# A last stage with TensorE in program order, DRAM writes issued by ScalarE, gelus kept in groups of four and four more early down tiles

## Chip, cores and metric

The kernel runs on one core of a Trainium2 chip. The metric is the device time of one execution in microseconds (us).

## What is computed

One decoder layer on 512 tokens of width 1024: a token mixer (mLSTM heads and sliding-window attention), cross-attention to 256 memory tokens, and a PEER layer with 16,384 single-neuron experts. Nearly all that matters here is the PEER layer. Cut to its core:

```python
qh = (xb @ w_pq).reshape(T, P_HEADS, 2, P_KEY_DIM)
s1 = einsum('thd,nd->thn', qh[:, :, 0], sub_keys1)
s2 = einsum('thd,nd->thn', qh[:, :, 1], sub_keys2)
v1, i1 = top_k(s1, 16); v2, i2 = top_k(s2, 16)
# best 16 of the 16 x 16 sums, per token and head
top_s, pos = top_k(cand_s, 16)
eidx = take_along_axis(cand_i, pos, -1)
g = softmax(top_s)
a = gelu(einsum('thkd,td->thk', expert_down[eidx], xb))
out = einsum('thkd,thk->td', expert_up[eidx], g * a)
```

A residual add and a final RMSNorm follow.

## The kernel before

The PEER layer is computed in two ways. For the first block of 128 tokens the kernel gathers the chosen rows of `expert_down` and `expert_up` with 256 indirect DMAs (`gather`, a Python generator that the code advances with `step`), and VectorE multiplies and sums them. The other three blocks (384 tokens) are computed densely, for all 16,384 experts in 128 tiles of 128:

- A **down tile** (class `Down`) loads 128 experts' weights (`draw`, two tiles per DMA), ScalarE casts them to a high part `dh`, VectorE subtracts to get a low part `dl`, TensorE runs 24 matmuls of 384 columns into `acc_d` (two PSUM buffers), and ScalarE takes the gelu.
- An **up tile** (`up_tile`, `up_mm`) loads the weights `uraw` (two tiles per DMA) and casts them to `uh` (ScalarE) and `ul` (VectorE). VectorE multiplies the gelu by the dense gates `wt` to get `cf`, which is split into `ch` (ScalarE) and `cl` (VectorE). TensorE runs 18 matmuls of 512 columns that add to six PSUM accumulators `acc_u` over all tiles. `uh`, `ul`, `ch` and `cl` have two buffers each.

Down tiles need only the layer's input, so `SP` = 68 of them are **early** (`Early.fill`): they are spread as filler for TensorE over the top-k (`peer_topk`, by the table `FRT`, and `FEND` columns at its end) and over `gating`, in which ScalarE and VectorE make one-hot matrices and TensorE multiplies them into the gates (`w`). The gelus of early tiles go to DRAM in groups of four (`gd<-gsp`) and come back later (`gsr<-gd`). The gates go to DRAM as eight writes of 2 MB (`wd<-stg`). In the kernel before, both kinds of writes are issued by SyncE, in one queue with the loads.

After gating `LEAD` = 5 down tiles are made, with 8 gather steps (`GLD`) among them. The **last stage** is the loop over `up_order()`: per up tile it first makes the down tiles that `made_by(u)` asks for, then the up tile, then some gather steps. Fresh gelus stay in a ring of 10 tiles. Then `finish` adds the residual, normalizes and writes out.

A scheduler of the framework sets each engine's order of instructions by its own timing model, within the data dependences and buffer counts. Each engine then runs its order strictly one after the other.

Of the kernel before, what the change touches and what calls it, by code (L numbers as in the profile page):

```python
# [11 lines left out]
F32 = mybir.dt.float32  # L12
# [9 lines left out]
P = 128  # L22
D = 1024
# [16 lines left out]

UG = 4
FRT = [16] + [20] * 14 + [24]
FEND = 3 * KT
FGT0 = KT
FGT = 3
SP = (sum(FRT) + FEND + FGT0 + (ND - NS) * 32 * FGT) // KT
# [2 lines left out]


GQ = range(9, 32, 2)
GLD = 8
GST = 122

LEAD = 5
RING = 10

# [604 lines left out]
def gating(c, early, ga):  # L664

    nc, ps, gs, mp = c.nc, c.ps, c.gs, c.mp
    V, A, T = nc.vector, nc.scalar, nc.tensor
    for b in range(NG + NS, NB):
        tr = []
        for n_, src in (("I1T", c.I1), ("I2T", c.I2), ("gT", c.gg)):  # L670
            tp = ps.tile([P, 512], F32, tag="a", name="tp_i")
            tr_ = T.transpose(tp[:, :P], src[:, b].rearrange("p h k -> p (h k)"), c.ident)
            o = gs.tile([P, P], F32, tag=n_, bufs=1, name=n_)
            A.copy(o, tp[:, :P])
            tr.append(o)
        i1, i2, g = tr
        n1 = gs.tile([P, P], F32, tag="n1", bufs=1, name="n1")
        A.mul(n1, i1, -1.0)
        io = c.iota.unsqueeze(1).to_broadcast([P, 4, P])

        def onehot(q):

            o1 = gs.tile([P, 4, P], F32, tag="oh1", bufs=5, name="oh1")
            ib = i1[:, 4 * q:4 * q + 4].unsqueeze(2).to_broadcast([P, 4, P])
            if q % 2:
                V.tensor_tensor(o1, io, ib, op=ALU.is_equal)
            else:
                for t1 in range(4):
                    t = 4 * q + t1
                    A.activation(o1[:, t1], c.iota, AF.Abs, bias=n1[:, t:t + 1])  # L690
                A.activation(o1, o1, AF.Relu, bias=1.0, scale=-1.0)
            return o1

        oh = [onehot(q) for q in range(3)]
        if b == NG + NS:
            with c.tc.issue_after(tr_.ins):
                early.fill(FGT0)
        for q in range(32):
            if q % 8 == 0:
                stg = gs.tile([P, NK, 32], F32, tag="stg", bufs=2, name="stg")  # L700
            if q + 3 < 32:
                oh.append(onehot(q + 3))
            o1 = oh[q]
            w = ps.tile([P, 512], F32, tag="b", name="w")
            w4 = w.rearrange("p (i t) -> p i t", t=4)
            for t1 in range(4):
                t = 4 * q + t1
                o2 = gs.tile([P, P], F32, tag="oh2", bufs=4, name="oh2")
                last = V.tensor_scalar(o2, c.iota, i2[:, t:t + 1], g[:, t:t + 1], op0=ALU.is_equal, op1=ALU.mult)
                mm = T.matmul(w4[:, :, t1], o1[:, t1], o2, start=True, stop=True)  # L710
            q8 = q % 8
            A.copy(stg[:, :, 4 * q8:4 * q8 + 4], w4)
            if q8 == 7:
                nc.sync.dma_start(c.wd[b - NG][:, :, 32 * UG * (q // 8):32 * UG * (q // 8 + 1)].rearrange("g p i -> p g i"),
                                  stg.rearrange("p (g i) t -> p g (i t)", i=UG))
            with c.tc.issue_after(mm.ins):
                early.fill(FGT)
            if b == NB - 1 and q in GQ:
                with c.tc.issue_after(c.sc[HD - 1][-1].ins), c.tc.issue_after(last.ins):
                    step(ga, 1)  # L720


def gather(c):

    nc, gp, mp = c.nc, c.gp, c.mp
    V, A, G = nc.vector, nc.scalar, nc.gpsimd
    dots = gp.tile([P, P], F32, name="dots")
    c.gacc = gp.tile([P, D], F32, name="gacc")

    def fetch(src, j):  # L730
        r = gp.tile([P, D], F32, tag="rows", bufs=8, name="rows")
        G.indirect_dma_start(out=r, out_offset=None, in_=src,  # L732
                             in_offset=bass.IndirectOffsetOnAxis(ap=c.eidx[:, j:j + 1], axis=0))
        return r

    for j in range(P):
        r = fetch(c.a["down_r"], j)
        V.tensor_tensor_reduce(r, r, c.xn0, 1.0, 0.0, op0=ALU.mult, op1=ALU.add, accum_out=dots[:, j:j + 1])  # L738
        yield
    coef = gp.tile([P, P], F32, name="coef")  # L740
    A.activation(coef, dots, AF.Gelu)
    V.tensor_tensor(coef, coef, c.gg[:, 0].rearrange("p h k -> p (h k)"), op=ALU.mult)
    for j in range(P):
        r = fetch(c.a["up"], j)
        if j == 0:
            V.tensor_scalar(c.gacc, r, coef[:, j:j + 1], None, op0=ALU.mult)
        else:
            V.scalar_tensor_tensor(c.gacc, r, coef[:, j:j + 1], c.gacc, op0=ALU.mult, op1=ALU.add)  # L748
        yield


def split3(c, pool, raw, tag, bufs):
    hi = pool.tile([P, D], F32R, tag=tag + "h", bufs=bufs, name=tag + "h")
    lo = pool.tile([P, D], F32R, tag=tag + "l", bufs=bufs, name=tag + "l")
    c.nc.scalar.copy(hi, raw)  # L755
    return hi, lo
# [25 lines left out]
class Down:  # L782
# [27 lines left out]
    def out(self):  # L810
        c = self.c
        i2 = self.i2
        if i2 >= SP:
            g = c.gl.tile([P, TD], F32, tag="gel", bufs=RING, name="gel")
            c.nc.scalar.activation(g, self.acc[:, :TD], AF.Gelu)
            return g
        if i2 % UG == 0:
            c.gsp = c.dp.tile([P, UG, TD], F32, tag="gsp", bufs=2, name="gsp")
        c.nc.scalar.activation(c.gsp[:, i2 % UG], self.acc[:, :TD], AF.Gelu)
        if i2 % UG == UG - 1:  # L820
            c.nc.sync.dma_start(c.gd[i2 // UG], c.gsp)
        return None


def up_tile(c, u, i2, gel, acc):
# [9 lines left out]
            c.gsr = c.gl.tile([P, UG, TD], F32, tag="gsr", bufs=2, name="gsr")  # L835
            nc.sync.dma_start(c.gsr, c.gd[i2 // UG])
    if i2 % GRP == 0:
        c.uraw = up.tile([P, GRP, D], F32, tag="uraw", bufs=2, name="uraw")
        nc.sync.dma_start(c.uraw, c.a["up"].rearrange("(i p) d -> p i d", p=P)[:, i2:i2 + GRP])
    g = c.gsr[:, i2 % UG] if i2 < SP else gel[i2]  # L840
    raw = c.uraw[:, i2 % GRP]
    last = u == NK - 1
    if last:
        z = c.xlo.rearrange("p k t -> p (k t)")
        hi, lo = z[:, 0:D], z[:, D:2 * D]
        A.copy(hi, raw)
    else:
        hi, lo = split3(c, up, raw, "u", 2)
    V.tensor_tensor(lo, raw, f32(hi), op=ALU.subtract)  # L849
    cf = up.tile([P, TD], F32, tag="cf", bufs=2, name="cf")  # L850
    if last:
        ch, cl = z[:, 2 * D:2 * D + TD], z[:, 3 * D:3 * D + TD]
    else:
        ch = up.tile([P, TD], F32R, tag="ch", bufs=2, name="ch")
        cl = up.tile([P, TD], F32R, tag="cl", bufs=2, name="cl")
    c.cf = V.tensor_tensor(cf.rearrange("p (b t) -> p b t", t=32), g.rearrange("p (b t) -> p b t", t=32),
                    c.wt.rearrange("p b (q i t) -> p (b q) i t", q=4, i=UG)[:, :, i2 % UG], op=ALU.mult)
    A.copy(ch, cf)  # L858
# [204 lines left out]
def body(tc, a, out, dbg=None):  # L1063
# [3 lines left out]
    with ExitStack() as st:  # L1067
        def pool(name, bufs=1, side="left", **k):
            return tc.tile_pool(name=name, bufs=bufs, side=side, reuse_waits="tile", **k)
# [45 lines left out]
        def ahead(n):  # L1115
            for _ in range(n):
                gel.append(Down(c, len(gel)).mm().out())
# [5 lines left out]
            ws.close()  # L1123
        c.gl = st.enter_context(pool("gels"))
        with pool("gather", side="right") as c.gp:
            ga = gather(c)
            with pool("gating") as c.gs:
                gating(c, early, ga)
            c.up = st.enter_context(pool("up"))
            assert len(gel) == SP  # L1130
            for n in range(LEAD):
                ahead(1)
                with tc.issue_after(c.dl.ins):
                    step(ga, GLD * (n + 1) // LEAD - GLD * n // LEAD)
            pst_ = [c.ps.tile([P, 512], F32, tag=t, name="acc_u") for t in "bbbbaa"]
            acc = [[pst_[2 * b], pst_[2 * b + 1]] for b in range(ND)]
            last = []
            g0 = len(GQ) + GLD

            due = [u + made_by(u) for u in range(-1, GST)]  # L1140
            rows = [(2 * P - g0) * (d - due[0]) // (due[-1] - due[0]) for d in due]
            rows += [rows[-1]] * (NK - GST)
            for u, i2 in enumerate(up_order()):
                ahead(made_by(u) - len(gel))
                parts = up_tile(c, u, i2, gel, acc)
                for i in range(rows[u + 1] - rows[u]):
                    with tc.issue_after((c.cf if i == 0 else c.cl).ins):
                        step(ga, 1)
                if u >= NK - 2:
                    last.append(parts)  # L1150
                else:
                    for b in range(ND):
                        up_mm(c, u, parts, acc, b)
            step(ga, 2 * P)
            c.hb = []
            for b in range(NB):
                c.hb.append(c.gp.tile([P, D], F32, tag="rows", bufs=8, name="hb"))
                nc.sync.dma_start(c.hb[b], c.hd[b])
            c.gfin = c.xn0
            nc.scalar.dma_start(c.gfin, a["prow"][0, 0:D].partition_broadcast(P))  # L1160
# [79 lines left out]
```

## Time and profile before

| | |
|---|---|
| runs of the kernel before | 1663.74 us median (1662.36 to 1670.41, three runs) |
| the profiled execution | 1663.32 us; its span from first to last instruction 1661.6 us |
| busy in the span | TensorE 97%, VectorE 74%, ScalarE 43%, GpSimd 36% |
| chain that ended last | TensorE 89%, VectorE 5% |
| mean granted TensorE clock | 0.992 |

The table is read thus: TensorE is almost always busy and nearly all of the chain runs through it, so a change can gain only what TensorE now waits or runs at a lower clock, some 3% at most, unless it removes matmuls. Which waits those are must be read stage by stage.

### The profile page before, as it was taken

Reading aid. Unit: us, or ns where it says so; the run is one execution under the profiler, and the core shown is the slowest. Engines: PE = TensorE matmul, PEld = TensorE weight load, DVE = VectorE, ACT = ScalarE, POOL = GpSimd, SP = SyncE. Lnnn points to the kernel's source line nnn. Section 1 sums busy time; section 2 is a strip of 40 time slices with the busy share of each in tenths; the row PEclk is TensorE's granted clock in tenths of the full one; section 3 lists DMA queues with packets and bytes.
Section 4 is the critical chain, followed back from the end, with each engine's and each line's share of the span. In section 5 each row is a group of like instructions: output and inputs, shape, how many; then the busy total and the mean of one; then the engine's idle time right before and its main releaser. Section 6 shows DMA issues by size and latency. Waiting matters only on the chain.

```text
span 1661.6 us, 22993 instructions
## 1 busy us (share of the span) xinstructions
PE 1613.3 (97%) x8367; PEld 1415.6 (85%) x8368; DVE 1224.1 (74%) x2686; ACT 722.1 (43%) x1209; POOL 599.1 (36%) x427
## 2 busy tenths in 40 slices
PE   7998899999999999999998999999999999999987
PEld 5766688878999999899997988888888888888865
DVE  5545565464787887877877778778778878887995
ACT  5435544343544454677743333333333333333333
POOL 2000000000027878877333244434434444443630
PEclk9999999999999999999999999999999999999998
DMA  5236135232255435678999989889899899987992
GB/s 214 76 127 253 62 116 178 76 152 106 96 166 146 115 71 140 178 197 223 376 306 406 348 311 368 321 335 348 314 357 366 296 353 357 342 326 260 394 368 101
DMA packets 149969, 400.58 MB, mean 241 GB/s; under 512 B 28240, under 2 KB 62176, under 8 KB 137440
## 3 DMA queue, kind: packets, MB, share of 16 engines
q1 hardware_dynamic: 90096, 255.76, 42.2%
q0 software_dynamic: 55360, 134.32, 24.3%
q10 hardware_dynamic: 4400, 9.04, 1.5%
q8 instruction: 65, 1.06, 0.3%
q14 instruction: 48, 0.39, 0.1%
HBM read 356.28 MB, written 42.80 MB: 240 GB/s over the span
## 4 chain that ended last, share of the span: by engine, by line
PE 89%; DVE 5%; issue 3%; ACT 2%; DMA 1%; POOL 0%; DVEq 0%; POOLq 0%; ACTq 0%
PE acc_d L806 10%; PE acc_d L805 10%; PE acc_d L804 10%; PE acc_u L871 9%; PE acc_u L872 9%; PE acc_u L870 9%; PE acc_f L970 4%; PE acc_f L972 4%; PE acc_f L971 4%; PE w L710 3%; PE acc_t L984 2%; PE acc_t L985 2%; PE acc_t L983 2%; DVE ul L849 1%; PE s L550 1%
## 5 line engine op out<-in xcount | busy, mean ns | idle before, releaser
L804 PE MATMUL acc_d<-xhi,dh 128*128 128x384 f32 x1024 | 351.2, 343 | 5.7 <-ACT dh L755 4.7
L806 PE MATMUL acc_d<-xhi,dl 128*128 128x384 f32 x1024 | 346.2, 338 | 1.7 <-DVE dl L793 1.7
L805 PE MATMUL acc_d<-xlo,dh 128*128 128x384 f32 x1024 | 344.9, 337 | 0.0
L871 PE MATMUL acc_u<-ul,ch 128*128 128x512 f32 x762 | 298.4, 392 | 2.7 <-DVE ul L849 2.7
L872 PE MATMUL acc_u<-uh,cl 128*128 128x512 f32 x762 | 297.7, 391 | 0.0
L655 POOL DMA_INDIRECT wd<-gg,ei x128 | 232.5, 1816 | 147.8 <-DVE ei L649 87.3
L732 POOL DMA_INDIRECT rows<-in_down_r_dram,eidx x128 | 166.7, 1302 | 258.6 <-DVE dots L738 241.3
L732 POOL DMA_INDIRECT rows<-in_up_dram,eidx x128 | 175.8, 1373 | 212.7 <-DVE gacc L748 187.8
L858 ACT CAST ch<-cf 128x384 fp32r<-128x384 f32 x127 | 65.3, 514 | 394.7 <-issue 213.0
L870 PE MATMUL acc_u<-uh,ch 128*128 128x512 f32 x762 | 217.0, 391 | 2.7 <-ACT uh L755 2.7
L793 DVE TENSOR_TENSOR dl<-draw,dh 128x1024 fp32r<-128x1024 f32 x128 | 155.9, 1219 | 81.6 <-ACT dh L755 78.6
L755 ACT CAST dh<-draw 128x1024 fp32r<-128x1024 f32 x128 | 134.0, 1049 | 161.7 <-PE acc_d L805 135.4
L804 PEld LDWEIGHTS acc_d<-xhi,dh 128*128 128x128 f32 x1024 | 194.2, 190 | 10.5 <-ACT dh L755 5.0
L806 PEld LDWEIGHTS acc_d<-xhi,dl 128*128 128x128 f32 x1024 | 193.6, 189 | 6.0 <-DVE dl L793 2.9
L805 PEld LDWEIGHTS acc_d<-xlo,dh 128*128 128x128 f32 x1024 | 193.9, 189 | 4.0
L871 PEld LDWEIGHTS acc_u<-ul,ch 128*128 128x128 f32 x762 | 143.0, 188 | 34.0 <-DVE ul L849 5.2
L870 PEld LDWEIGHTS acc_u<-uh,ch 128*128 128x128 f32 x762 | 142.1, 188 | 30.1 <-ACT uh L755 3.6
L872 PEld LDWEIGHTS acc_u<-uh,cl 128*128 128x128 f32 x762 | 143.1, 188 | 28.5
L748 DVE SCALAR_TENSOR_TENSOR gacc<-rows,coef,gacc 128x1024 f32<-128x1024 f32 x127 | 162.0, 1276 | 0.4
L849 DVE TENSOR_TENSOR ul<-uraw,uh 128x1024 fp32r<-128x1024 f32 x127 | 154.1, 1218 | 2.9 <-ACT uh L755 2.1
L738 DVE CUSTOM_DVE_ANT_0 rows<-rows,xn 128x1024 f32<-128x1024 f32 x128 | 154.5, 1218 | 0.0
L859 DVE TENSOR_TENSOR cl<-cf,ch 128x384 fp32r<-128x384 f32 x127 | 70.3, 554 | 113.8 <-ACT ch L858 113.6
(333 smaller groups left out, 2620.4 us busy)
## 6 DMA issues: line engine op xcount, KB each, us to landing
draw<-in_down_t_dram SPq DMA_DIRECT2D x64, 1024.0 KB, 7.7
uraw<-in_up_dram SPq DMA_DIRECT2D x64, 1024.0 KB, 8.3
wt<-wd SPq DMA_DIRECT2D x96, 256.0 KB, 8.4
wd<-stg SPq DMA_DIRECT2D x8, 2048.0 KB, 11.8
gd<-gsp SPq DMA_DIRECT2D x17, 768.0 KB, 4.1
gsr<-gd SPq DMA_DIRECT2D x17, 768.0 KB, 11.2
wd<-zero ACTq DMA_DIRECT2D x1, 8192.0 KB, 26.4
raw<-in_w_pq_dram SPq DMA_DIRECT2D x8, 1024.0 KB, 4.8
```

Of the source, the lines that this page charges most:

```text
L655: i = G.indirect_dma_start(out=out, out_offset=bass.IndirectOffsetOnAxis(ap=ei[:, h, k:k + 1], axis=0), in_=c.gg[:, NG, hh, k:k + 1], in_o ...
L732: G.indirect_dma_start(out=r, out_offset=None, in_=src, in_offset=bass.IndirectOffsetOnAxis(ap=c.eidx[:, j:j + 1], axis=0))
L738: V.tensor_tensor_reduce(r, r, c.xn0, 1.0, 0.0, op0=ALU.mult, op1=ALU.add, accum_out=dots[:, j:j + 1])
L748: V.scalar_tensor_tensor(c.gacc, r, coef[:, j:j + 1], c.gacc, op0=ALU.mult, op1=ALU.add)
L793: c.dl = nc.vector.tensor_tensor(self.lo, raw, f32(self.hi), op=ALU.subtract)
L804: T.matmul(acc[:, :TD], self.hi[:, ks], c.xhi[:, k, NG * P:], start=(k == 0), stop=False)
L805: T.matmul(acc[:, :TD], self.hi[:, ks], c.xlo[:, k, NG * P:], start=False, stop=False)
L806: T.matmul(acc[:, :TD], self.lo[:, ks], c.xhi[:, k, NG * P:], start=False, stop=(k == KT - 1))
L849: V.tensor_tensor(lo, raw, f32(hi), op=ALU.subtract)
L870: T.matmul(acc[b][n], ch[:, t], hi[:, d], start=st, stop=False)
L871: T.matmul(acc[b][n], ch[:, t], lo[:, d], start=False, stop=False)
L872: T.matmul(acc[b][n], cl[:, t], hi[:, d], start=False, stop=sp)
```

## The change

It does five things.

1. In the loop of the last stage TensorE's instructions keep the order in which the code is written (`manual_schedule` for PE); the other engines are scheduled as before. `uh`, `ul`, `ch` and `cl` get three buffers.
2. The writes `gd<-gsp` and `wd<-stg` are issued by ScalarE instead of SyncE.
3. Fresh gelus are stored in tiles of four; of three consecutive groups two take the buffers of `gsp` and one a buffer of its own.
4. `FEND` goes from 24 to 56: four more early down tiles at the end of the top-k, four fewer later (`SP` 72).
5. The 8 gather steps among the five `LEAD` tiles move into the loop, where the steps are spread with weights 3 per up tile and 5 per down tile. Gather rows have 7 buffers instead of 8, the indices of these steps are a copy (`rowid`) made after the `LEAD` tiles, and the first two `uraw` loads are issued ahead of the `LEAD` tiles.

```diff
-FEND = 3 * KT
+FEND = 7 * KT
...
-GLD = 8
+WST, WTL = 3, 5
-RING = 10
...
-                nc.sync.dma_start(c.wd[b - NG][:, :, 32 * UG * (q // 8):32 * UG * (q // 8 + 1)].rearrange("g p i -> p g i"),
+                nc.scalar.dma_start(c.wd[b - NG][:, :, 32 * UG * (q // 8):32 * UG * (q // 8 + 1)].rearrange("g p i -> p g i"),
...
-        r = gp.tile([P, D], F32, tag="rows", bufs=8, name="rows")
+        r = gp.tile([P, D], F32, tag="rows", bufs=7, name="rows")
-                             in_offset=bass.IndirectOffsetOnAxis(ap=c.eidx[:, j:j + 1], axis=0))
+                             in_offset=bass.IndirectOffsetOnAxis(ap=c.rowid[:, j:j + 1], axis=0))
...
-            g = c.gl.tile([P, TD], F32, tag="gel", bufs=RING, name="gel")
+            n = (i2 - SP) // UG
+            if i2 % UG == 0:
+                if n % 3 == 2:
+                    c.gel = c.gl.tile([P, UG, TD], F32, tag="gel", bufs=1, name="gel")
+                else:
+                    c.gel = c.dp.tile([P, UG, TD], F32, tag="gsp", bufs=2, name="gel")
+            g = c.gel[:, i2 % UG]
...
-            c.nc.sync.dma_start(c.gd[i2 // UG], c.gsp)
+            c.nc.scalar.dma_start(c.gd[i2 // UG], c.gsp)
...
-        hi, lo = split3(c, up, raw, "u", 2)
+        hi, lo = split3(c, up, raw, "u", 3)
...
-        ch = up.tile([P, TD], F32R, tag="ch", bufs=2, name="ch")
-        cl = up.tile([P, TD], F32R, tag="cl", bufs=2, name="cl")
+        ch = up.tile([P, TD], F32R, tag="ch", bufs=3, name="ch")
+        cl = up.tile([P, TD], F32R, tag="cl", bufs=3, name="cl")
...
-            for n in range(LEAD):
-                ahead(1)
-                with tc.issue_after(c.dl.ins):
-                    step(ga, GLD * (n + 1) // LEAD - GLD * n // LEAD)
+            c.ur = {i2: up_load(c, i2) for i2 in up_order()[0:2 * GRP:GRP]}
+            ahead(LEAD)
+            c.rowid = c.gp.tile([P, P], I32, name="rowid")
+            with tc.issue_after(c.dl.ins):
+                nc.vector.tensor_copy(c.rowid, c.eidx)
...
-            due = [u + made_by(u) for u in range(-1, GST)]
+            due = [WST * u + WTL * made_by(u) for u in range(-1, GST)]
...
-            for u, i2 in enumerate(up_order()):
+            with tc.manual_schedule(engines={mybir.EngineType.PE}):
+                for u, i2 in enumerate(up_order()):
```

How the instructions move is seen in each engine's order. Three places follow; the numbers are those of the buffers' tiles. Line numbers are those of each kernel's own file.

**TensorE, at the border of two up tiles in the last stage.** Before, from the 118th to the 119th up tile; the 119th has the weights `uh_14413`, `ul_14414`:

```order
L871 MATMUL acc_u_8592<-ul_14378,ch_14382 128x512
L872 MATMUL acc_u_8592<-uh_14377,cl_14383 128x512
L870 MATMUL acc_u_8587<-uh_14413,ch_14418 128x512
L870 MATMUL acc_u_8588<-uh_14413,ch_14418 128x512
L870 MATMUL acc_u_8589<-uh_14413,ch_14418 128x512
L870 MATMUL acc_u_8590<-uh_14413,ch_14418 128x512
L870 MATMUL acc_u_8591<-uh_14413,ch_14418 128x512
L870 MATMUL acc_u_8592<-uh_14413,ch_14418 128x512
L871 MATMUL acc_u_8587<-ul_14414,ch_14418 128x512
```

In the change, from the 40th to the 41st up tile (`uh_10684`, `ul_10685`):

```order
L882 MATMUL acc_u_8697<-ul_10648,ch_10652 128x512
L883 MATMUL acc_u_8697<-uh_10647,cl_10653 128x512
L881 MATMUL acc_u_8692<-uh_10684,ch_10689 128x512
L882 MATMUL acc_u_8692<-ul_10685,ch_10689 128x512
L883 MATMUL acc_u_8692<-uh_10684,cl_10690 128x512
L881 MATMUL acc_u_8693<-uh_10684,ch_10689 128x512
```

Six matmuls with `uh` used to stand before the first that needs `ul`; now one does. In the loop down tiles now stand whole between up tiles, one after two or three up tiles, where they used to be cut into pieces. (At the end of the top-k, the first transposes of gating, `tp_i`, stand behind three whole down tiles instead of one, and three more stand between them and the first `w`.)

**ScalarE, at the same borders.** Before (`ch_14485` is for the 120th up tile):

```order
L755 CAST uh_14377<-uraw_14310 128x1024
L858 CAST ch_14418<-cf_14417 128x384
L858 CAST ch_14485<-cf_14484 128x384
L755 CAST uh_14413<-uraw_14411 128x1024
L755 CAST uh_14480<-uraw_14411 128x1024
```

In the change (`ch_10791` is for the 43rd up tile; `gel_10497` is the gelu of the down tile ahead of the 39th):

```order
L754 CAST uh_10647<-uraw_10608 128x1024
L869 CAST ch_10689<-cf_10688 128x384
L754 CAST dh_10820<-draw_10715 128x1024
L821 ACTIVATE gel_10497<-acc_d_10582 128x384
L869 CAST ch_10752<-cf_10751 128x384
L869 CAST ch_10791<-cf_10790 128x384
L754 CAST uh_10684<-uraw_10682 128x1024
L754 CAST uh_10747<-uraw_10682 128x1024
```

Both orders have a `ch` ahead of a `uh` of an earlier up tile. Before, that `ch` reuses the buffer of the up tile two earlier, the 118th, in the change that of the one three earlier, the 40th.

**SyncE before and ScalarE in the change, from the last 2 MB write of gates to the first up tiles.** Before, SyncE:

```order
L790 DMA draw_8475<-in_down_t_dram 128x2048
L714 DMA wd2_69<-stg_8165 128x32x128
L821 DMA gd_70<-gsp_8160 128x1536
L790 DMA draw_8548<-in_down_t_dram 128x2048
L831 DMA wt_8593<-wd0_67 128x512
```

In the change, ScalarE (`gel_8563<-acc_d_8538` is the gelu of the first `LEAD` tile):

```order
L713 DMA wd2_69<-stg_8291 128x32x128
L754 CAST dh_8565<-draw_8532 128x1024
L825 ACTIVATE gsp_8286<-acc_d_8462 128x384
L754 CAST dh_8597<-draw_8595 128x1024
L827 DMA gd_70<-gsp_8286 128x1536
L821 ACTIVATE gel_8563<-acc_d_8538 128x384
L754 CAST dh_8627<-draw_8595 128x1024
```

The two writes have left SyncE's queue, so the loads there follow each other directly; on ScalarE the casts and gelus of the `LEAD` tiles now stand behind them.

## Rows read from the trace of the kernel before

**Rows 1.** The page: the span, and TensorE's line of part 1.

```profile
span 1661.6 us, 22993 instructions
PE 1613.3 (97%) x8367; PEld 1415.6 (85%) x8368; DVE 1224.1 (74%) x2686; ACT 722.1 (43%) x1209; POOL 599.1 (36%) x427
```

**Rows 2.** Windows: stretch, sum, busy by engine, granted clock, DMA share, GB/s.

```profile
690.00:695.00 5.00, 4.75 (x19) 4.51 (x20) 2.88 (x11) 4.56 (x17) 4.39 (x3) 0.66 1.05 371
850.00:890.00 40.00, 33.45 (x174) 31.85 (x173) 25.45 (x41) 12.67 (x20) 15.40 (x12) 0.91 0.93 337
890.00:1545.00 655.00, 655.00 (x3171) 577.91 (x3170) 522.95 (x673) 229.74 (x318) 268.63 (x202) 1.00 0.90 337
1545.00:1645.00 100.00, 94.56 (x408) 75.73 (x407) 88.28 (x106) 34.32 (x49) 37.48 (x25) 1.00 0.80 310
```

**Rows 3.** Waits of TensorE: us in total, times, longest.

```profile
PE acc_u L870 <- ACT uh L755: 2.7, 2, 1.4
...
PE acc_u L871 <- DVE ul L849: 2.7, 4, 0.9
```

**Rows 4.** Timeline of TensorE, end of the top-k: start, us, engine, line, work.

```profile
679.04 0.44 PE L806 MATMUL acc_d<-xhi,dl 128*128 128x384 f32 x1 [0.79 <-DVE dl L793]
...
686.95 0.34 PE L806 MATMUL acc_d<-xhi,dl 128*128 128x384 f32 x1
...
690.70 0.67 PE L804 MATMUL acc_d<-xhi,dh 128*128 128x384 f32 x1
```

**Rows 5.** Timeline of SyncE's queue, ScalarE and TensorE, the five lead tiles.

```profile
856.53 0.42 PE L804 MATMUL acc_d<-xhi,dh 128*128 128x384 f32 x1
...
857.43 0.38 SPq L714 DMA_DIRECT2D wd<-stg  x1
859.66 5.23 SPq L821 DMA_DIRECT2D gd<-gsp  x1
864.99 1.00 SPq L790 DMA_DIRECT2D draw<-in_down_t_dram  x1
...
869.68 0.33 PE L804 MATMUL acc_d<-xhi,dh 128*128 128x384 f32 x1
...
872.63 0.34 PE L806 MATMUL acc_d<-xhi,dl 128*128 128x384 f32 x1
...
876.54 1.99 ACT L755 CAST dh<-draw 128x1024 fp32r<-128x1024 f32 x2 [7.20 <-DMA draw<-in_down_t_dram]
...
877.63 0.44 PE L804 MATMUL acc_d<-xhi,dh 128*128 128x384 f32 x1 [4.66 <-ACT dh L755]
...
889.80 1.55 PE L870 MATMUL acc_u<-uh,ch 128*128 128x512 f32 x6
```

**Rows 6.** Timeline of TensorE, end of the last stage.

```profile
1586.68 0.39 PE L872 MATMUL acc_u<-uh,cl 128*128 128x512 f32 x1
1588.43 1.65 PE L870 MATMUL acc_u<-uh,ch 128*128 128x512 f32 x6 [1.37 <-ACT uh L755]
1591.03 0.50 PE L871 MATMUL acc_u<-ul,ch 128*128 128x512 f32 x1 [0.95 <-DVE ul L849]
...
1593.90 1.52 PE L870 MATMUL acc_u<-uh,ch 128*128 128x512 f32 x6
...
1597.98 1.52 PE L870 MATMUL acc_u<-uh,ch 128*128 128x512 f32 x6
```

**Rows 7.** Groups by line, ScalarE and VectorE, 890 to 1545 us: busy, mean ns.

```profile
L755 ACT CAST uh<-uraw 128x1024 fp32r<-128x1024 f32 x104 | 107.8, 1048 | 0.0
...
L858 ACT CAST ch<-cf 128x384 fp32r<-128x384 f32 x104 | 53.5, 514 | 334.8 <-issue 175.6 <-PE acc_u L871 158.3 <-ACT uh L755 0.9
L815 ACT ACTIVATE gel<-acc_d 128x384 f32<-128x384 f32 x55 | 26.5, 482 | 18.1 <-DVE cf L856 15.7 <-PE acc_d L806 2.4
...
L849 DVE TENSOR_TENSOR ul<-uraw,uh 128x1024 fp32r<-128x1024 f32 x105 | 127.4, 1219 | 2.5 <-ACT uh L755 1.8
```

**Rows 8.** Timeline of SyncE's queue in gating, the longest hold of a write.

```profile
803.30 5.83 SPq L821 DMA_DIRECT2D gd<-gsp  x1
```

## The prediction before the run

> **What bounds the kernel now.** The page comes first: TensorE is busy 1613.3 us of a span of 1661.6 [rows 1], so 48 us without matmuls are all that waits can give back; the reader should see there that no other engine is near its limit. Then windows, stage by stage [rows 2]. From 890 to 1545 us, most of the last stage, TensorE is busy 655.00 of 655.00 us at full clock: nothing to gain there. VectorE does 522.95 us in the same stretch (80%), and the DMA engines are 0.90 busy at 337 GB/s. The waits lie around it: 850 to 890 has 6.55 us without a matmul and a clock of 0.91, 1545 to 1645 has 5.44 us. A third, short one is where the top-k ends; there the clock fell to 0.66 [rows 2]. I read what ended these waits, and then the timelines.
>
> *End of the last stage.* TensorE waited twice for `uh`, 2.7 us, and four times for `ul`, 2.7 us [rows 3]. The timeline shows one such stop [rows 6]: an up tile ends with the matmul at 1586.68; the next begins at 1588.43 and reaches its first `ul` at 1591.03. Undisturbed, 18 matmuls take 4.08 us (1593.90 to 1597.98), 0.227 us each. So 1588.43 is 1.52 us late, the six matmuls to 1591.03 lost another 1.24, the twelve to 1593.90 0.15: 2.9 us. The orders explain it: `ch` of the 120th tile waits for the buffer of the 118th, thus for the end of that tile's matmuls, and `uh` of the 119th stands behind it. There are two such borders with no down tile between (the 114th and the 118th tile), hence 5.8 us; the other two waits for `ul` are what the 2.7 leave beside two of 0.95, 0.8, with restarts 1.2. **Lost: 7.0 us.**
>
> *Lead tiles.* From 856.53 to 889.80 [rows 5] TensorE runs 131 down matmuls (11 to end the early tiles, 5 x 24). 17 steps from 869.68 to 872.63 give 0.1735 us each, so 22.7 us would do and 33.3 passed: **lost 10.6 us**. The largest wait, 4.66 us before 877.63, goes back to a load issued at 864.99 whose cast starts at 876.54; it stood in SyncE's queue behind a `gd` write whose issue took 5.23 us, itself 2.2 us behind a 2 MB `wd` write.
>
> *End of the top-k.* Between 686.95 and 690.70 only three transposes ran, about 3.3 us lost; 0.79 us waiting for `dl` at 679.04 [rows 4]; and 1.7 us of clock, 0.34 of 5 us [rows 2]. **Lost 5.8 us.**
>
> **The change, part by part.** No matmul is added; TensorE's work is the same.
>
> *Four more early tiles.* 96 matmuls, 16.7 us, go from the loop to the end of the top-k. Two of the tiles stand ahead of the first transposes and cover 8.3 us. Their two `dl` go ahead of the transposes' data on VectorE and delay these by 2.4 us at 1219 ns each (`ul`, the same shape [rows 7]): 3.3 + 2.4 is covered. Their casts and loads have the same two buffers as now; one `dl` late as at 679.04 would cost 0.8. I take 0.6 left: **-5.2**. Bounds: -5.8, and -2 if `dl` comes late three times and the clock falls again. One more group of gelus is written and read, 0.8 MB each way: hidden while the DMA share stays at 0.90. If that cover goes, one late load costs what the lead tiles show, 4.7.
>
> *Writes issued by ScalarE.* The loads of the lead tiles no longer stand behind the write; SyncE's queue holds only loads there. The 4.66 us wait should go. What is late next, by the orders: the `ch` of the first up tile stands behind the gelu of the last lead tile, with nothing for TensorE between. At least gelu and `ch`, 0.48 + 0.51 = 1.0 us. At most the chain from the end of the fourth lead tile: `dh`, gelu, one `uh`, three `ul` (VectorE has them ahead of the first `cf`), `ch`: 1.05 + 0.48 + 1.05 + 3.66 + 0.51 = 6.8 us [rows 7], against 24 x 0.1735 = 4.2 of the fifth tile: 2.6. I take the upper end, as every step of it is fixed by the orders, and 0.5 for a `dl` that is late among the lead tiles, as the one at 679.04: 3.1 of 10.6 stay, **-7.5**. Bounds: -9.6 and -2.
>
> The writes now hold ScalarE where they held SyncE. Behind each stand casts, gelus and copies for TensorE. The longest hold seen is 5.83 us [rows 8], the last 5.23 [rows 5]. In the order of the change four `gd` writes follow a `wd` write within three blocks of gating. Bounds: 0, since `dh` is made a tile ahead and `w` has four PSUM buffers, and 4 x 5.8 = 23. I take **+2**, nearer to 0: in each of the four places the next cast is already done when the write is issued.
>
> The Trainium skill, DMA: Bandwidth & Descriptors, section Issuing engines are not separate DMA queues, speaks against a gain: DMAs of all issuing engines run on the same 16 DMA engines, and another issuer saves only issue time, "usually small". Here that issue time was 5.23 us, so the row makes it a term; by the rule alone the sum would lack it and end near 1661.
>
> *TensorE in program order, three buffers.* The two borders and the two `ul` waits go: -7.0. Three new borders of the kind come, from the 40th, 72nd and 104th up tile to the next: `ch` of three tiles ahead stands before `uh` of the next, no down tile lies between, and now one matmul instead of six precedes the first `ul`. Each: 1.52 as measured, then `ul` 1.22 less 0.23, 0.15 to restart, 2.7 us; three are 8.1. Bounds: 1.7 each, and 3.9 where a gather step is ahead of `ul`. Where an up or a down tile lies between, its 4.1 us cover the chain `ch`, `uh`, `ul` of 2.8; some of those may be short by a few tenths, 0.5 in all. **+1.6**, between -2 and +6.
>
> *Edits costed at nothing.* A group of gelus is reused at least nine up tiles after its last use, so the gelu never waits. Eight gather steps more in the loop are 8 x 1.22, less four `dl`: 4.9 us for VectorE, which has 20% free; if that goes, every `ul` is late. Rows start later with one buffer less; TensorE waits for none of them.
>
> **Sum**: -5.2 - 7.5 + 2 + 1.6 = -9.1, from the profiled execution's 1663.32: **1654 us**. That execution lies 0.4 below the median of 1663.74, so the sum holds for the median too. About 0.5% (8.3 us) is what a measurement of this kernel tells from no change: below 1655.4 is faster, above 1672.1 slower.
>
> **Rivals.**
> *ScalarE held by its own writes (slower).* All four holds reach TensorE whole: 23 instead of 2, so 1675. For it: both measured holds come with a `wd` write just ahead, as in the order of the change. Against: SyncE's were held in the second half of gating, and what is ready ahead must run out first. It is slower than before from about 20 us of passed-on holds.
> *The queue doesn't matter.* The load lands late anyway, since the DMA engines are busy: 0.93 from 850 to 890 [rows 2]. The lead tiles keep their loss: 1654 + 7.5, about 1661. For it: the load took 11.5 us from issue to cast. Against: those were added to a late issue. This is what the rule would make of it; by the trace, less likely.
> *The last stage stops more often.* Without pieces of down tiles as filler each late `uraw` load stops TensorE at once. Two or three stops like that at 877.63, or `ul` behind gather steps at each border, give 6: 1660. For it: a DMA share of 0.90. Against: no wait in 655 us, and now three tiles of lead.
> *Everything is covered.* Holds 0, first up tile 1.0, borders 1.7 each: 1654 - 2 - 2 - 3, near 1647.
>
> **How the numbers follow.** Forecast (1650 to 1658) 0.45, of which 0.37 is below 1655.4; stops in the last stage 0.23; the queue doesn't matter 0.12; all covered 0.12; ScalarE held 0.08. Faster 0.37 + 0.12 = 0.49; same 0.08 + 0.23 + 0.12 = 0.43; slower 0.08. The range 1645 to 1665 leaves out the slower case and the tails of two others, under 2 in 10.
>
> **What would show it.** Right: no wait of TensorE ahead of the transposes; no late `draw` in the lead tiles, some 2.6 us before the first up tile; in the last stage three stops of `uh` then `ul`, some 190 us apart (32 up tiles with their down tiles), none near the end. Wrong: TensorE waiting in gating behind a `gd` issue of ScalarE, or waits for `uh` after a late `uraw`. The prediction fails if the window of the last stage is no longer full outside the three stops.

## The result and the profile after

| | before | change |
|---|---|---|
| median of 13 runs each | 1663.63 us | 1675.03 us (1670.94 to 1682.74) |
| ratio | | 1.0074 [1.0061, 1.0087] |
| profiled execution, its span | 1663.32, 1661.6 us | 1674.29, 1672.6 us |

The change is slower by 11.4 us; 1654 was forecast. The span grew by 11.0 us while TensorE's busy time stayed (1613.3 in [rows 1]).

The page of the change, the span and TensorE's line:

```profile
span 1672.6 us, 22889 instructions
PE 1611.8 (96%) x8367; PEld 1415.5 (85%) x8368; DVE 1230.9 (74%) x2687; ACT 721.8 (43%) x1209; POOL 599.4 (36%) x427
```

Windows of the change (columns as in [rows 2]):

```profile
690.00:695.00 5.00, 5.00 (x31) 5.00 (x30) 2.15 (x9) 1.44 (x2) 4.39 (x3) 1.00 1.10 389
750.00:800.00 50.00, 47.63 (x331) 47.44 (x329) 33.70 (x90) 32.30 (x74) 37.10 (x23) 1.00 0.89 256
800.00:850.00 50.00, 42.28 (x277) 42.15 (x278) 37.75 (x96) 37.36 (x83) 5.73 (x5) 0.90 0.76 251
900.00:920.00 20.00, 12.21 (x50) 10.13 (x49) 10.96 (x18) 6.02 (x10) 6.06 (x6) 0.83 1.03 410
890.00:1545.00 655.00, 639.73 (x3048) 559.14 (x3047) 537.13 (x699) 227.51 (x313) 293.06 (x215) 0.99 0.94 355
1545.00:1645.00 100.00, 100.00 (x471) 86.40 (x470) 89.10 (x101) 35.18 (x52) 36.86 (x30) 1.00 0.85 313
```

The three weak places of [rows 2] moved. The end of the top-k (690) and the end of the last stage (1545) are now full. New holes stand in the middle of gating (10.1 us without a matmul in 750 to 850, clock 0.90), before the first up tile (7.8 us in 900 to 920, clock 0.83) and inside the last stage, which used to be full. Waits of TensorE from 600 us on (columns as in [rows 3]) name them:

```profile
PE w L709 <- DVE oh L708: 10.1, 1, 10.1
PE acc_u L881 <- ACT ch L869: 7.8, 1, 7.8
PE acc_u L881 <- ACT uh L754: 4.1, 3, 1.4
PE acc_u L882 <- DVE ul L860: 3.4, 7, 0.9
```

**Gating.** The timeline of ScalarE, then of VectorE, then of TensorE, in the change:

```profile
786.47 0.38 ACTq L713 DMA_DIRECT2D wd<-stg  x1
...
788.96 13.30 ACTq L827 DMA_DIRECT2D gd<-gsp  x1
...
802.31 0.58 ACT L711 COPY stg<-w 128x512 f32<-128x512 f32 x1 [12.39 <-issue]
...
805.10 1.05 ACT L754 CAST dh<-draw 128x1024 fp32r<-128x1024 f32 x1
...
806.18 1.23 DVE L792 TENSOR_TENSOR dl<-draw,dh 128x1024 fp32r<-128x1024 f32 x1 [10.58 <-ACT dh L754]
...
797.03 0.61 PE L709 MATMUL w<-oh,oh 128*128 128x128 f32 x4
807.72 1.22 PE L709 MATMUL w<-oh,oh 128*128 128x128 f32 x4 [10.08 <-DVE oh L708]
```

The `gd` write was handed to ScalarE's queue 2.5 us after a 2 MB `wd` write, and its issue held ScalarE for 13.30 us. Everything behind it, copies, one-hot matrices and the next `dh`, stood still. The releaser named is VectorE's `oh`; but VectorE itself waited 10.6 us for the `dh` cast of 805.10, so the wait must be followed one step further, to the hold. TensorE lived 8 us on what was ready and then stopped for 10.1; its next matmuls ran at a lower clock (granted 0.90 from 800 to 850 us).

**The first up tile.** The chain that ended last runs there over two transfers, and then the stop on TensorE:

```profile
880.48 17.57 DMA wd<-stg
...
898.12 8.57 DMA wt<-wd
...
906.81 0.57 DVE cf L867
```

```profile
907.97 0.79 PE L881 MATMUL acc_u<-uh,ch 128*128 128x512 f32 x1 [7.79 <-ACT ch L869]
```

The last gates go to DRAM and come back: 26.3 us from the issue of the last `wd` write to the first `cf`. Five lead tiles cover 20.8 of it.

**A ledger.** Four points exist in both programs: first and last gate matmul, first up matmul, last matmul. The groups by line show them (times of the first and the last start), before and in the change (the last matmul starts at 1649.9 and 1660.8):

```profile
L710 PE MATMUL w<-oh,oh x512: 270/275/308, 696.6 to 856.5; 128*128 128x128 f32 x171
L870 PE MATMUL acc_u<-uh,ch x762: 387/389/500, 889.8 to 1643.1; 128*128 128x512 f32 x191
```

```profile
L709 PE MATMUL w<-oh,oh x512: 272/275/582, 708.6 to 879.5; 128*128 128x128 f32 x171
L881 PE MATMUL acc_u<-uh,ch x762: 387/389/792, 908.0 to 1654.0; 128*128 128x512 f32 x191
```

The change has 96, 89, 72 and 0 more down matmuls ahead of these points by the orders; at 0.1735 us each these are taken off. What is left, change less before, is the time lost so far: -4.7, +7.6, +5.7, +10.9. By stage, against the four terms of the prediction:

| stage | predicted | change |
|---|---|---|
| to the first gate matmul | -5.2 | -4.7 |
| gating (holds of ScalarE) | +2 | +12.3 |
| lead tiles to the first up matmul | -7.5 | -1.9 |
| last stage | +1.6 | +5.2 |
| sum | -9.1 | +10.9 |

### The profile page after: what moved, and what is told of

It is laid out like the page before. It is cut to its first block, busy times and chain, and to the rows that moved or that the text cites. A ratio compares the mean times of both kernels' runs of the same rounds, so it can differ in the third digit from the quotient of the medians.

```text
span 1672.6 us, 22889 instructions
## 1 busy us (share of the span) xinstructions
PE 1611.8 (96%) x8367; PEld 1415.5 (85%) x8368; DVE 1230.9 (74%) x2687; ACT 721.8 (43%) x1209; POOL 599.4 (36%) x427
## 4 chain that ended last, share of the span: by engine, by line
PE 90%; DVE 4%; DMA 2%; ACT 2%; issue 1%; SPq 0%; DVEq 0%; POOLq 0%; POOL 0%; ACTq 0%
PE acc_u L882 10%; PE acc_u L883 10%; PE acc_u L881 10%; PE acc_d L804 10%; PE acc_d L803 10%; PE acc_d L805 10%; PE acc_f L981 4%; PE acc_f L983 4%; PE acc_f L982 4%; PE w L709 3%; PE acc_t L995 2%; PE acc_t L996 2%; PE acc_t L994 2%; DMA wd<-stg 1%; PE s L549 1%
## 5 line engine op out<-in xcount | busy, mean ns | idle before, releaser
L881 PE MATMUL acc_u<-uh,ch 128*128 128x512 f32 x762 | 297.8, 392 | 11.9 <-ACT ch L869 7.8
L731 POOL DMA_INDIRECT rows<-in_down_r_dram,rowid x116 | 159.4, 1374 | 241.5 <-DVE dots L737 179.7
L731 POOL DMA_INDIRECT rows<-in_up_dram,rowid x128 | 169.9, 1328 | 207.3 <-DVE gacc L747 187.1
L754 ACT CAST uh<-uraw 128x1024 fp32r<-128x1024 f32 x127 | 128.0, 1046 | 0.8 <-DMA wd<-stg 0.8
```

Source lines behind the costliest of these rows:

```text
L731: G.indirect_dma_start(out=r, out_offset=None, in_=src, in_offset=bass.IndirectOffsetOnAxis(ap=c.rowid[:, j:j + 1], axis=0))
L881: T.matmul(acc[b][n], ch[:, t], hi[:, d], start=st, stop=False)
```

## Experiments

The ledger was made for every profiled execution; at its first point those with the four early tiles stand at -5.0 to -3.0 and those without at 0 to +1.8, so 2 us are noise there. One, uh_first_lead6's, stands at +2.1; it took 6.4 us more than its median. A border is counted in the orders: a place where a `ch` stands on ScalarE ahead of the `uh` of an earlier up tile and TensorE has no matmul in between.

**gd_on_sync: which write holds.**

```diff
-            c.nc.scalar.dma_start(c.gd[i2 // UG], c.gsp)
+            c.nc.sync.dma_start(c.gd[i2 // UG], c.gsp)
```

> Only the small writes of gelus (gd) go back to SyncE; the 2 MB writes of gates (wd) stay on ScalarE, and the orders of TensorE and VectorE are those of the changed kernel. Theory (queue): a write is held until the 2 MB write ahead of it in the same engine's queue has mostly drained, up to about 16 us after that one's issue. Then no gd and no wd issue is held now (all under 0.5 us on either engine), the stop of 10 us in gating is gone with its slow clock, about 12 us in all, and the time is near 1662. Rival (backlog): the hold follows the load on the DMA engines, whoever issued the 2 MB write. Then gd is held on SyncE by 5 to 13 us, and the draw loads behind it come late as in the kernel before: gating is free of stops but the lead tiles lose some 5 us, near 1667. In both, the stop of 7.8 us before the first up tile stays.

Measured 1665.81 us, ratio to before 1.0015 [1.0005, 1.0024]. All `gd` issues of this run (min/median/max ns), TensorE's wait, and the chain ahead of the first up tile:

```profile
L827 SPq DMA_DIRECT2D gd<-gsp x18: 320/327/383, 433.7 to 870.3; - x18
```

```profile
PE acc_u L881 <- ACT ch L869: 10.1, 1, 10.1
```

```profile
868.10 22.37 DMA wd<-stg
```

No write is held on either engine, and gating is full (ledger -4.5, -4.7, -4.4, +1.5). A `gd` write is again issued 2.5 us behind a `wd` write, which landed only after 23.8 us; on the other queue it was not held. So the queue theory holds, and the backlog rival falls. It is some 4 us slower than expected; 2.3 of that is the stop before the first up tile, which grew, since the last `wd` write landed after 22.4 us.

**wd_on_sync and both_on_sync.** Only the 2 MB writes, then both kinds, back on SyncE.

```diff
-                nc.scalar.dma_start(c.wd[b - NG]...
+                nc.sync.dma_start(c.wd[b - NG]...
```

> The other half: only the 2 MB writes (wd) go back to SyncE, the gelu writes (gd) stay on ScalarE. Theory (queue): ScalarE's queue holds no 2 MB write, so no gd is held; ScalarE is free, and gating has no stop; but the loads of SyncE that stand within some 16 us behind a wd write are held by up to 7 us. Near 1662 to 1665. Rival (backlog): gd is held on ScalarE by about 13 us once and 3.5 once, as in the changed kernel, and the time stays near 1674.

> Both kinds of writes back on SyncE; the rest of the change stays. Theory: gating loses nothing; in the lead tiles the loads are held behind the last wd and gd write by about 5 us as before, so TensorE stops some 4.7 us there and less before the first up tile, whose gates land some 25 us after the last wd write either way. Without the gating stop near 1662. Rival (the stop in gating comes from the four early tiles or the moved loads, not from the queue): the 10 us stay, near 1674.

Measured 1656.28 (ratio 0.9957 [0.9941, 0.9972]) and 1656.98 us (0.9961 [0.9946, 0.9976]). With `wd` on SyncE, the `gd` issues on ScalarE and the `draw` issues on SyncE:

```profile
L827 ACTq DMA_DIRECT2D gd<-gsp x18: 326/326/327, 433.7 to 870.5; - x18
...
L789 SPq DMA_DIRECT2D draw<-in_down_t_dram x64: 327/333/10375, 359.0 to 1507.1; - x64
```

The hold went to the queue that carries `wd`: in wd_on_sync a load of SyncE is held 10.4 us, in both_on_sync a `gd` write 10.06, and TensorE does not feel it in gating. Both runs are better than expected, because the stop before the first up tile shrank as well, to 1.8 and 1.9 us: the last `wd` write lands after 11.4 and 8.7 us here. So in the order of the change moving the writes costs 1675.03 - 1656.98 = 18 us, and all else in the change gains 6.7. The two profiled executions are 20.3 us apart at the last matmul; by the ledger of both_on_sync (-3.0, -2.7, -8.2, -9.4) gating accounts for 12.0 of it, the lead tiles for 3.6, and the last stage for 6.4 (1.7 go off for the first point), where the scheduler's order had three borders in the change and has two here.

**queue_only.** The kernel before with the two writes issued by ScalarE, nothing else.

> The kernel before with both kinds of writes issued by ScalarE and nothing else; its orders of TensorE stay, but for 14 rows. Theory (queue): two gd writes stand 2.5 us behind a wd write, as in the change; one of them holds ScalarE for some 13 us in gating and stops TensorE for about 10, and the last wd, which no longer holds back the loads of SyncE, lands some 20 us after its issue. The lead tiles lose less for their loads, up to 5 us. 1663.7 + 12 - 5 + 3: near 1674, 1668 to 1680. Rival: the holds hurt only in the order of the change (four early tiles more, loads ahead of the lead tiles): within 4 us of 1663.7.

Measured 1670.37 us (1665.73 to 1677.62), ratio 1.0038 [1.0021, 1.0055]. The `gd` issues, the landing of the eight `wd` writes, and the last of these alone:

```profile
L821 ACTq DMA_DIRECT2D gd<-gsp x17: 326/326/11017, 435.3 to 870.4; - x17
```

```profile
DMA to landing us min/median/max: 10.2/12.9/23.9
...
wd<-stg ACTq DMA_DIRECT2D x1, 2048.0 KB, 20.1
```

The move alone costs 6.9 us here, against 18 in the order of the change. A long hold comes in the old order too, 11.0 us, but not where it was expected: the two `gd` writes that stand 2.5 and 2.2 us behind a `wd` write were held 3.64 and 4.09 us, and the long hold fell on one 9.1 us behind the fifth `wd` write, which landed after 23.9 us. The last `wd` write is late as expected, 20.1 us. The ledger of its profiled execution (+1.8, +10.8, +8.5, +12.8), which took 6.3 us more than the median, puts the loss into gating (9.0), as in the change.

**loads_later: why the last write lands late on ScalarE's queue.** gd_on_sync without the early `uraw` loads; on SyncE these now stand behind the `wt` loads, which wait for the last `wd` write.

```diff
-            c.ur = {i2: up_load(c, i2) for i2 in up_order()[0:2 * GRP:GRP]}
             ahead(LEAD)
+            c.ur = {}
```

> The change with only the gelu writes on SyncE (measured 1665.8; its last 2 MB write, issued by ScalarE, landed 22.4 us after its issue), and the first two uraw loads no longer ahead of the lead tiles: in SyncE's queue they now stand behind the wt loads, which wait for that write. The three borders of the last stage stay. Theory (competition): the last write was slow because SyncE's loads ran beside it; without 2 MB of uraw it lands after 11 to 15 us; uraw then comes late instead, so the first up tile still waits some 6 to 9 us and the time is 1663 to 1666. Rival (the queue of ScalarE is slow in itself): it still lands after 17 us or more, and with uraw behind it the first up tile waits 15 us or more: 1670 or above.

Measured 1669.53 us. The last `wd` write in this run (KB, us to landing):

```profile
wd<-stg ACTq DMA_DIRECT2D x1, 2048.0 KB, 16.4
```

It fell from 22.4 to 16.4 us, between the two theories' bounds, and the time lies between them too. The fall can't be put down to the `uraw` loads alone: while the last write was under way GpSimd's gathers moved 1.15 MB in gd_on_sync and nothing here, and the fifth `wd` write, which this edit does not touch, landed after 20.8 us there and after 12.9 here. The run is slower than gd_on_sync, although the first up tile waits less, 6.6 us, and now for `uh`, since `uraw` comes late: the ledger (-4.9, -5.2, -8.3, +5.3) puts the loss behind the first up matmul, where a second stop for `uh` follows, 2.3 us, and the matmuls are slow after all three borders.

**early_only.** The kernel before with `FEND = 7 * KT`.

> The kernel before with the four more early tiles at the end of the top-k and nothing else. Theory: the ledger at the first gate matmul gave -4.7 us for this part, and it stands alone: near 1659. Rival (given back): the tiles come out of the last stage, where they were filler between up tiles, and what is gained returns there as waits for uh or ul: near 1663.

Measured 1668.73 us, ratio 1.0029 [1.0018, 1.0040]: slower. TensorE's waits (before: 2.7 us, 2 times, and 2.7, 4 times [rows 3]):

```profile
PE acc_u L870 <- ACT uh L755: 6.8, 5, 1.4
PE acc_u L871 <- DVE ul L849: 6.2, 6, 2.0
```

The gain is there (-3.2 at the first gate matmul, -5.1 at the first up matmul), but the scheduler's new order has five borders in place of two, and the last stage loses 10.2: three more at 3.4 us. The rival was right, and went further than it said.

**three_early_less.** wd_on_sync with `FEND = 3 * KT`.

> The change with the 2 MB writes on SyncE, but with the old 24 columns at the end of the top-k instead of 56. Theory: the stop ahead of the first transposes returns, +4.7, and the order has one border without cover instead of two, -3 to -4: near 1657. Rival (the four early tiles are worth nothing, as the run with them alone was slower): -3 to -4 only, near 1653.

Measured 1654.64 us, ratio 0.9940 [0.9919, 0.9960], between the two. TensorE's waits show the old stop before the transposes again, and one border:

```profile
PE tp_i L671 <- DVE iu L644: 2.6, 1, 2.6
...
PE acc_u L881 <- ACT uh L754: 1.4, 1, 1.4
```

The last stage stands at -4.4 here. The early tiles are worth what was predicted where they stand; what decides is how many borders the new order happens to get, and at how many of them TensorE's clock falls (below).

**fill_in_loop.** wd_on_sync without `manual_schedule`.

> The change with the 2 MB writes on SyncE, but without the program order on TensorE: the scheduler may again cut down tiles into pieces between up tiles; three buffers stay. By the orders there are four borders without cover instead of two, all behind the 103rd up tile. Theory (borders): two more at 2.9 us, less 0.9 for the six matmuls ahead of the first ul in the old two, so +4: near 1660. Rival (pieces as filler are worth more than the borders cost): faster than 1656.

Measured 1656.49 us, ratio 0.9954 [0.9935, 0.9973]: the same as wd_on_sync, where 1660 was expected. There are four stops for `uh`, as the order has borders; three are the usual 1.4 us and one is 2.4:

```profile
PE acc_u L881 <- ACT uh L754: 6.5, 4, 2.4
```

The scheduler also put a sixth down tile ahead of the first up tile, which removed the 1.8 us there. Program order on TensorE, with all that follows from it in the other orders, is worth nothing that these runs can tell.

**uh_first, and two versions of it.** wd_on_sync with each `ch` ordered behind its tile's `uh`, and `cl` behind `ul`; then `LEAD = 6`; then also `GST = 116`.

```diff
...
-    A.copy(ch, cf)
-    c.cl = V.tensor_tensor(cl, cf, f32(ch), op=ALU.subtract)
+    with c.tc.issue_after(uh.ins):
+        A.copy(ch, cf)
+    with c.tc.issue_after(ul.ins):
+        c.cl = V.tensor_tensor(cl, cf, f32(ch), op=ALU.subtract)
```

> The change with the 2 MB writes on SyncE (measured 1656.3), and each ch and cl is ordered behind the uh and ul of its own up tile. By the orders the two borders at which a ch stands ahead of a uh of an earlier up tile, with no matmul between, are gone (the changed kernel has three, the kernel before two, the one with only early tiles five). Theory (borders): each cost 2.25 us of stop and up to 1.5 of slow clock, so -5 to -7: 1649 to 1651. Rival (program order): TensorE has nothing to fill a late cast with, and the stops move to other up tiles, whose ch now waits for its uh: within 2 us of 1656.

> The run with uh ordered first (measured 1654.15) and six lead tiles instead of five. Theory: the first up tile's wait of 1.9 us and its slow first matmuls, 1.5 us, are covered by 4.2 us more of down matmuls, -3: near 1651. Rival: the gates' way through DRAM and the loads move with the sixth tile's load, the wait stays, within 1 us of 1654.

> As the last, and the gather steps end at the 116th up tile instead of the 122nd, because with uh first VectorE was busy 29.9 of 30 us before the end and the time from the last matmul to the end had grown from 12.7 to 14.7 us. Theory: -2 more at the end: near 1649. Rival: the steps now crowd the loop, where VectorE has 15 to 20% free, and ul comes late: no gain, 1651 or above.

Measured 1654.15 (ratio 0.9935 [0.9917, 0.9954]), 1651.78 (0.9923 [0.9904, 0.9943]) and 1652.26 us (0.9930 [0.9910, 0.9951]). In uh_first no wait for `uh` is left; `ul`, `cl` and the first `ch` remain:

```profile
PE acc_u L885 <- DVE ul L861: 1.9, 4, 1.3
PE acc_u L884 <- ACT ch L871: 1.9, 1, 1.9
...
PE acc_u L886 <- DVE cl L873: 0.6, 1, 0.6
```

Only 2.1 of the expected 5 to 7 us came. By the ledger the last matmul was 3.5 us earlier than in wd_on_sync, but the scheduler put the last matmuls of all six accumulators at the very end, and VectorE had to wait for them; the timeline of TensorE and VectorE there:

```profile
1636.75 1.52 PE L886 MATMUL acc_u<-xlo 128*128 128x512 f32 x6
1637.18 3.68 DVE L897 TENSOR_TENSOR hb<-hb,acc_u 128x512 f32<-128x512 f32 x6 [1.99 <-PE acc_u L886]
```

So VectorE's load of gather steps was not what made the end longer, as I had written, and ending the steps earlier (`GST`) gained nothing. The sixth lead tile gained 2.4 us of the 3 expected by the medians; with four and six runs, and intervals of the two ratios that overlap, that gain is not clear of noise. At 1651.8 us this version beats both kernels.

## Why the prediction was wrong, step by step

- **End of the top-k, right**: -4.7 for -5.2; the window from 690 is full and its clock 1.00.
- **"Writes issued by ScalarE", +2: the step that failed.** +12.3 in gating, 10.1 of it the stop and the rest slow matmuls behind it. It went by the length of a write's own row, 5.83 us [rows 8], and reasoned that the next cast was already done. SyncE's queue in the kernel before shows what this price leaves out, the `wd` write ahead of it, and two more holds:

```profile
777.06 3.51 SPq L821 DMA_DIRECT2D gd<-gsp  x1
...
794.19 0.38 SPq L714 DMA_DIRECT2D wd<-stg  x1
803.30 5.83 SPq L821 DMA_DIRECT2D gd<-gsp  x1
...
834.08 6.96 SPq L790 DMA_DIRECT2D draw<-in_down_t_dram  x1
```

  The longest hold was not 5.83 but 6.96 us, of a load right behind a `wd` write. The hold of 5.83 ended at 809.13, 14.9 us after that `wd` write was issued; in the change 802.26 - 786.47 = 15.8. The 5.83 was only what was left when `gd` came; a `gd` that comes 2.5 us behind can be held 13. Not one cast had to be covered but all that ScalarE does in that time. Of the four places the prediction counted, one held 13.30 and one 3.52 us; the other two `gd` writes came 9.1 us behind and were not held. The Trainium skill, DMA: Bandwidth & Descriptors, section Issuing engines are not separate DMA queues, calls the time to initiate a DMA usually small beside the transfer. The trace disagrees here: 13.30 us of issue.

  Distance alone does not give the length: the `gd` write 2.5 us behind the fourth `wd` write was held 3.51 us before (777.06) and 13.30 in the change. What differed is the data that moved beside that `wd` write. GpSimd's queue, which carries the gathers, in the first 10 us after the issue of the fourth `wd` write before, of the fifth before, and of the fourth in the change (packets, MB, share of 16 engines):

```profile
q0 software_dynamic: 569, 0.00, 10.0%
...
q0 software_dynamic: 673, 2.43, 61.9%
...
q0 software_dynamic: 468, 1.69, 50.0%
```

  These writes landed after 9.1, 18.0 and 19.3 us. The first gather is issued at 784.1 us before and at 783.1 in the change, but the four early tiles put gating 12 us later, so that the gathers now meet the fourth write. The runs bear this out: with the early tiles alone (early_only) that `gd` write is held 11.77 us, on SyncE; with the move alone (queue_only) 3.64, and the long hold comes behind the fifth. That the gathers are what slows the `wd` write is read from these rows; no run moves them alone.
- **Lead tiles, -7.5**: -1.9. The late `draw` load went as said. What the step named as late next, the gelu of the last lead tile (at most 2.6), was not it: the chain `wd` to DRAM, `wt` back, `cf` takes 26.3 us and the prediction never listed it; in the kernel before the lost 10.6 us [rows 5] covered it. On SyncE's queue the same step gives -5.7 (wd_on_sync), near the forecast; there `uraw` releases the first up tile, not the gates.
- **Last stage, +1.6**: the old borders went, the three new ones came, at 4.1 us for `uh` and three of the seven `ul` waits; mechanism right, size off. The third one:

```profile
1533.22 0.39 PE L883 MATMUL acc_u<-uh,cl 128*128 128x512 f32 x1
1534.97 0.49 PE L881 MATMUL acc_u<-uh,ch 128*128 128x512 f32 x1 [1.37 <-ACT uh L754]
1536.34 0.79 PE L882 MATMUL acc_u<-ul,ch 128*128 128x512 f32 x1 [0.88 <-DVE ul L860]
...
1539.50 0.46 PE L883 MATMUL acc_u<-uh,cl 128*128 128x512 f32 x1
1539.79 0.39 PE L881 MATMUL acc_u<-uh,ch 128*128 128x512 f32 x1
```

  The granted clock there, and the other engines (columns as in [rows 2]):

```profile
1534.00:1540.00 6.00, 4.15 (x10) 3.10 (x11) 5.93 (x7) 2.81 (x3) 3.33 (x3) 0.72 0.96 324
```

  The tenth matmul was due at 1533.22 + 10 x 0.2266 = 1535.49 and starts at 1539.79: 4.3 us, not the predicted 2.7. The other 1.6 is the clock, 0.72 over these 6 us: after the stop the matmuls come 0.427 us apart, for 0.227. Two of the three borders had it, and the first up tile too (1.8 us). The formula of the prediction, -7.0 + 2.7 for each border + 0.5, gives -3.8, -1.1 and +1.6 for one, two and three; measured were -4.4, then -1.2 and +1.9, then +5.2 and +5.9. both_on_sync (-1.2) and wd_on_sync (+1.9) have the same two borders; the slow matmuls came at neither of them in the first and at both in the second.
- **Which rival came.** "ScalarE held by its own writes" named the mechanism, holds that reach TensorE, though as four of 5.8 us; it was one of 13.3. That its time (1675) is the measured one is luck: gating lost 12.3 us and not 23, and the lead tiles (5.6) and the last stage (3.6), which it left as forecast, made up for it. "The queue doesn't matter" fell: the queue decides 18 us in this order and 6.9 in the old one.

## What to carry to other kernels

Before a write is moved to an engine that computes, look at what stands ahead of it in that engine's queue, and read a hold from the issue of the large transfer in front to the end of the held issue, not from the held row. Look also at what other queues move while that transfer drains, and whether another part of the change shifts the two against each other. When a wait is removed, list every chain that it covered, transfers through DRAM too, with their issue and landing times. Where a scheduler sets the order, count the bad places in the new order for every part of the change: an edit that gains where it stands (-3 to -5 us here) can lose twice that elsewhere.

## What the runs showed of the hardware

The same 2 MB write, the last of gating, landed 8.7, 10.4 and 11.4 us after its issue on SyncE's queue (both_on_sync, before, wd_on_sync), where the loads behind it are held, and 16.4 to 22.4 us on ScalarE's (loads_later, the change, queue_only, gd_on_sync), where SyncE's loads run beside it. Until it landed all queues together moved 2.3 to 3.2 MB in the first three and 4.5 to 7.7 MB in the others, at 268 to 345 GB/s. ScalarE's queue is not needed for a late landing: where the gathers run, one `wd` write on SyncE's queue took 17.7 to 18.3 us in each of the same three runs, with 6.2 to 6.6 MB moved. A write that stays longer also lets more pass beside it, so that the other traffic is the cause is argued, not shown. The Trainium skill, same page, section Queues, rings and completion order, says that each DMA engine takes turns between queues packet by packet; writes of small packets would then lose against loads of large ones. The traces agree in direction; the runs don't show the turns themselves.

The hold is a property of the queue: with `wd` on ScalarE no issue of `gd` or of a load on SyncE took over 1.5 us (gd_on_sync), while behind `wd` in the same queue the issues held over 1.5 us ended between 5.7 us (both_on_sync) and 20.1 us (queue_only) after its own.
